# A two-layer hybrid attention trunk on one core: the second attention's low halves moved behind the matmul steps, two of its queries moved forward, and the residual's loads held back

## The chip, the core and the metric

The kernel runs on one core of a Trainium2 chip. TensorE (PE) multiplies, and its weight loads (PEld) overlap its matmuls; VectorE (DVE) and ScalarE (ACT) do the elementwise work; GpSimd (POOL) and SyncE (SP) mostly issue DMAs, and so does ACT. The metric is device time in microseconds (us). Before the change the median of three runs is 1460.07 us (1458.28 to 1465.57).

## The reference

The input is x of 512 tokens by 1024, in float32. Each of two layers computes

```
h    = rmsnorm(x) ;  proj = h @ w_in                 # queries, keys, values, gates
y_a  = forgetting_attention(q_a, k_a, v_a, f_a) @ w_o_fox        # 8 heads of 64
o_c, o_s, o_w = sparse_attention(q_b, compressed, selected, window keys and values)
y_b  = (g0 * o_c + g1 * o_s + g2 * o_w) @ w_o_nsa                # 8 heads, 2 key heads
x    = x + (sigmoid(gate_a) * y_a + sigmoid(gate_b) * y_b) @ w_out
x    = x + square(relu(rmsnorm(x) @ w_up)) @ w_down
```

and a last rmsnorm follows. Both attentions are causal. With 512 tokens the selected branch takes all eight blocks and the window covers everything, so both are plain causal attentions over different keys. Queries and the second attention's keys have a rotation of 16 of their 64 dimensions.

## The kernel before

Activations lie transposed, 128 features by 512 tokens a tile. Products in float32 are split: each operand becomes a high half (a cast) and a low half (the rest), and three matmuls give a product. A weight block of 128x1024 is fetched to `raw` (L173), cast to `wh` on ACT (L189), its low half `wl` is formed on DVE (L190), and `gemm` runs 24 matmuls of 512 columns on it (L219 to L221), six to a step; after each step the generator yields, so that other work can be put between steps. Two raw tiles and two of each half are in rotation. `order` lists all weight blocks in the order of their use. Which queue fetches them is `self.queue`: SP's, except in the second attention, where it is POOL's.

A layer goes: token projections; the first attention (`attend`), filled with the remaining projections (`fill1`: the keys and queries of the first attention, then a compression of keys and values run in turns with the rest, which ends with the selected keys `ks`, the window keys `kw`, and the first and second queries of the second attention); the second attention (`attend_pairs`); the mixing (the second output projection and the gates); the output projection, which adds x; the MLP.

The second attention is what the change touches. It has eight pairs: for each of four head pairs first the selected branch (kind 0), then the window branch (kind 1). A pair's scores (`pair_scores`) go over four row blocks, the longest first: `prepare` scales the previous block's probabilities and writes their high halves as float16 (ACT, L613); two products with the keys follow, one for each head (PE, L640), each followed by a masked maximum on DVE (L555) and an exponential on ACT (L557); `finish` forms the low halves (DVE, L618) and issues transposing DMAs on SP's queue (L623), from the half buffer `EE` to tiles `PT`. A pair later `pair_values` multiplies `PT` with the values (PE, L666 and L683). `after` adds the compressed branch and evicts (L1182 to L1191).

`attend_pairs` writes the order out by hand. Each pair has four rounds; in a round the scores advance by two yields (one block of rows), in the last two rounds the previous pair's values go out, and then `fill` advances by `rate` steps (2 in a round; 2.5 in the first pair's rounds, 3 behind the last pair). The last part of a kind 0 pair (block 0, `late`) is taken at the start of the next pair. `fill` is `fill2`: the gates' projections (a gate's product with the norm's factor on DVE, L1213, and a tanh, L1214), the first output projection, each half block of which is folded into `MA` on DVE (`ma`, L1223), and the raw projections of the third and fourth queries (`parted`). `timed` puts two more things at numbered steps: the compressed branch's probabilities (`cmp_probs`, whose last step forms `cp`, L941) and `turned(2)` and `turned(3)`, which rotate and split those two queries on DVE and ACT and copy them to `q2` by DMAs (L410).

PE's order in the stage is pinned to the order of the code. The chain of softmax, prepare and finish is tied, in code order, on DVE and on ACT. `yield_to_chain` ties each round's other DVE work (gates, `ma`, weights, `cp`) behind the last chain instruction that the round emitted before it. The rest is left to the build's scheduler.

Tiles come from pools with fixed counts: `t2` has 13 buffers (probabilities of the short rows, `PT`, `cp`, later x), `hl` one (the split keys, and the fourth row block's probabilities). The first query's copies and the selected keys' go out on SP's queue, the window keys' on POOL's. At the end of the stage the eight tiles of x are loaded on ACT's queue (L1279); nothing ties them to a place there.

## Time and profile before

| | |
|---|---|
| profiled execution | 1462.19 us; span 1460.1 us; mean granted TensorE clock 0.990 |
| busy in the span | PE 1423.4 us, DVE 1192.8 us, ACT 922.4 us, POOL 170.8 us |
| second attention, layer 0 / layer 1 | about 167 to 338 us / 889 to 1058 us |
| DVE, median of one instruction | L618 612 ns; L941 689 ns |
| transposing DMAs (L623) | 96, median issue 1278 ns |

A group line of the profile names line, engine, operation and tiles (out<-in), then how often it ran. A wait line reads: engine, what it wanted to write and its line, then who released it, with the total, the number of waits and the longest. A line of the chain gives start, duration and who was the last to hold things up; "issue" is time in which the engine waited for nothing that the profile shows. A row of the table of windows gives the stretch, its length, then busy time and instructions of PE, PEld, DVE, ACT and POOL, the granted clock, the DMA engines' share and GB/s.

### The profile page before, as it was taken

To read this page: it belongs to the slowest core of one execution; us is meant where nothing else is said; L and a number is where in the kernel's file an instruction comes from. 1 tells how busy PE (TensorE), PEld (TensorE's weight loads), DVE (VectorE), ACT (ScalarE), POOL (GpSimd) and SP (SyncE) were. 2 spreads that over 40 slices of the span, in tenths; PEclk is the share of its full clock that TensorE was granted. 3 is DMA by queue.
4 is the path that set the end of the run, shared out by engine and by line. 5 is a ranking of instruction groups with operands and counts; after the bars stand their busy time and mean duration, and the time that the engine had idled before them with its cause. 6 is when DMAs were issued, how large, how long until landed. Compare 5 with 4: busy or idle time off the path is not lost.

```text
span 1460.1 us, 23049 instructions
## 1 busy us (share of the span) xinstructions
PE 1423.4 (97%) x7948; PEld 1217.7 (83%) x7948; DVE 1192.8 (82%) x2522; ACT 922.4 (63%) x1907; POOL 170.8 (12%) x249
## 2 busy tenths in 40 slices
PE   9999999999999999999999999998899999999997
PEld 8877777777898999989888787776688989899896
DVE  6587888866889898989866878988478888989898
ACT  6375576753677575848454756767437776758485
POOL 2000101000011111111300011010000111111112
PEclk9999999999999999999999999999999999999999
DMA  7564668584558676777835646576833575766674
GB/s 254 167 158 138 152 148 157 129 158 144 154 133 197 167 180 165 193 170 202 266 134 166 180 117 167 130 159 130 167 109 114 148 182 137 197 174 176 160 213 116
DMA packets 163956, 237.67 MB, mean 163 GB/s; under 512 B 95104, under 2 KB 95488, under 8 KB 163840
## 3 DMA queue, kind: packets, MB, share of 16 engines
q1 hardware_dynamic: 137200, 162.78, 39.0%
q0 software_dynamic: 23904, 68.69, 23.2%
q10 hardware_dynamic: 2736, 4.74, 1.7%
q8 instruction: 62, 1.02, 0.3%
q14 instruction: 54, 0.44, 0.1%
HBM read 168.46 MB, written 6.29 MB: 120 GB/s over the span
## 4 chain that ended last, share of the span: by engine, by line
PE 80%; DVE 7%; DMA 5%; ACT 4%; issue 2%; SPq 0%; POOL 0%; ACTq 0%; POOLq 0%
PE ps_mm L1849 7%; PE ps_S L1849 7%; PE ps_mm L219 7%; PE ps_mm L221 7%; PE ps_mm L220 7%; PE ps_S L1722 6%; PE ps_PT L1722 6%; PE ps_mm L1722 6%; DMA PT<-EE 3%; PE ps_O L1849 3%; PE ps_PT L1849 3%; PE ps_O L1722 3%; DVE EE L618 1%; DMA q<-qs 1%; ACT EE L613 1%
## 5 line engine op out<-in xcount | busy, mean ns | idle before, releaser
L219 PE MATMUL ps_mm<-uh,wh 128*128 128x512 f32 x480 | 196.3, 409 | 16.1 <-DVE ma L1223 8.1
L221 PE MATMUL ps_mm<-uh,wl 128*128 128x512 f32 x480 | 192.1, 400 | 0.2
L220 PE MATMUL ps_mm<-ul,wh 128*128 128x512 f32 x480 | 191.2, 398 | 0.0
L189 ACT CAST wh<-raw 128x1024 fp32r<-128x1024 f32 (+2 forms) x111 | 112.4, 1013 | 116.8 <-PE ps_mm L220 41.0
L190 DVE TENSOR_TENSOR wl<-raw,wh 128x1024 fp32r<-128x1024 f32 (+2 forms) x111 | 130.4, 1176 | 38.7 <-ACT wh L189 38.3
L1831 ACT CAST sh<-raw 128x512 fp32r<-128x512 f32 x160 | 96.7, 619 | 76.2 <-DMA raw<-wt 28.0
L219 PEld LDWEIGHTS ps_mm<-uh,wh 128*128 128x128 f32 x480 | 91.8, 191 | 36.8 <-ACT wh L189 8.8
L1839 DVE TENSOR_TENSOR sl<-raw,sh 128x512 fp32r<-128x512 f32 x160 | 106.2, 684 | 18.7 <-ACT sh L1831 18.6
L221 PEld LDWEIGHTS ps_mm<-uh,wl 128*128 128x128 f32 x480 | 92.0, 192 | 21.0 <-DVE wl L190 1.6
L220 PEld LDWEIGHTS ps_mm<-ul,wh 128*128 128x128 f32 x480 | 92.4, 192 | 16.1
L1689 DVE TENSOR_TENSOR sl<-raw,sh 128x512 fp32r<-128x512 f32 x128 | 83.8, 684 | 5.2 <-ACT sh L1675 4.0
L613 ACT ACTIVATE EE<-E,rr 128x512 f16<-128x512 f32 (+3 forms) x112 | 59.3, 576 | 44.2 <-DVE rr L607 19.3
L1722 PE MATMUL ps_S<-t,sh 128*128 128x256 f32 x384 | 83.3, 283 | 1.0 <-ACT yz L1774 0.9
L1675 ACT CAST sh<-raw 128x512 fp32r<-128x512 f32 x128 | 75.2, 617 | 4.4 <-DVE sl L1839 4.4
L1675 ACT CAST sh<-sx 128x512 fp32r<-128x512 f32 x96 | 58.2, 613 | 26.6 <-DVE sx L1657 24.7
L1689 DVE TENSOR_TENSOR sl<-sx,sh 128x512 fp32r<-128x512 f32 x96 | 64.5, 684 | 12.6 <-ACT sh L1675 12.6
L557 ACT ACTIVATE E<-E,mx 128x512 f32<-128x512 f32 (+3 forms) x112 | 64.3, 575 | 15.1 <-DVE mx L555 14.7
L1722 PE MATMUL ps_S<-t,sl 128*128 128x256 f32 x256 | 72.0, 281 | 0.0
L618 DVE SCALAR_TENSOR_TENSOR EE<-E,rr,EE 128x512 f16<-128x512 f32 (+3 forms) x112 | 60.0, 575 | 11.9 <-ACT EE L613 11.6
L1696 POOL DMA_DIRECT2D raw<-raw x32 | 28.0, 874 | 342.8 <-DVE sl L1689 92.8
L219 PE MATMUL ps_mm<-oh,wh 128*128 128x512 f32 x160 | 63.6, 397 | 1.5 <-DVE gate L1213 1.2
L1825 POOL DMA_DIRECT2D raw<-wt x48 | 42.0, 879 | 195.2 <-DVE k_t L1597 87.6
(480 smaller groups left out, 4374.6 us busy)
## 6 DMA issues: line engine op xcount, KB each, us to landing
raw<-wup SPq DMA_DIRECT2D x64, 512.0 KB
raw<-wt POOLq DMA_DIRECT2D x48, 512.0 KB, 7.0
raw<-wb SPq DMA_DIRECT2D x35, 512.0 KB
raw<-wt SPq DMA_DIRECT2D x32, 512.0 KB
sx<-wt SPq DMA_DIRECT2D x64, 256.0 KB
raw<-wb POOLq DMA_DIRECT2D x29, 512.0 KB, 4.9
kd<-hl SPq DMA_DIRECT2D x40, 256.0 KB
w<-w SPq DMA_DIRECT2D x32, 256.0 KB
```

Of the source, the lines that this page charges most:

```text
L189: nc.scalar.copy(h[:, :n], raw[:, :n])
L190: nc.vector.tensor_tensor(lo[:, :n], raw[:, :n], h[:, :n].bitcast(F32), op=OP.subtract)
L219: mm(ps, h[:, c], xh, start=start and i == 0, stop=False)
L220: mm(ps, h[:, c], xl, start=False, stop=False)
L221: mm(ps, lo[:, c], xh, start=False, stop=stop and i == ks - 1)
L618: nc.vector.scalar_tensor_tensor(out[1], x, f, out[0], op0=OP.mult, op1=OP.subtract)
L1675: self.nc.scalar.copy(h, self.source(k, i))
L1689: self.nc.vector.tensor_tensor(lo, self.source(k, i), h.bitcast(F32), op=OP.subtract)
L1722: self.nc.tensor.matmul(ps, w, x, skip_group_check=True, **kw)
L1831: self.nc.scalar.copy(h, self.operand(d, i, p))
L1839: self.nc.vector.tensor_tensor(lo, self.operand(d, i, p), h.bitcast(F32), op=OP.subtract)
L1849: self.nc.tensor.matmul(ps[t][:, cols], a[:, s], m, start=new and f == 0, stop=f == 2, skip_group_check=True)
```

## The change

1. In `pair_scores` each row block yields once more ahead of `finish`. `attend_pairs` advances the scores by two as before, then the fill, and only then by one more, which runs `finish`. So the low halves and the transposes are emitted behind the round's gemm steps, and the steps' DVE work is no longer tied behind them. The same holds for the end of `late` and for the last round of a pair.
2. `fill1` takes the first query's projection ahead of `ks` and `kw`. The first pair's rows (`early`) come from `t2` rather than `hl`.
3. In `fill2` the third query's projection comes behind the first two gate blocks and their half blocks, `gated(0)`, instead of behind `gated(2)`, and `turned(2)` goes from steps 30, 32, 34 to 18, 22, 24.
4. x's loads are tied behind the last ACT instruction of `attend_pairs`. The weights' queue returns to SP's after the mixing rather than ahead of it.

```diff
--- before.py
+++ after.py
@@ -559,10 +559,13 @@
 
     def pair_rows(self, P):
 
-        X = [self.t("t2", [128, T], name="E") for _ in range(2)]
-        two = [self.t("t2", [128, T], name="E") for _ in range(2)]
-        three = self.t("hl", [128, 2, T], name="E")
-        E = [[X[e][:, :128], X[e][:, 128:384], two[e][:, :384], three[:, e]] for e in range(2)]
+        if P.get("early"):
+            three, two, X = ([self.t("t2", [128, T], name="E") for _ in range(2)] for _ in range(3))
+        else:
+            X, two = ([self.t("t2", [128, T], name="E") for _ in range(2)] for _ in range(2))
+            three = self.t("hl", [128, 2, T], name="E")
+            three = [three[:, e] for e in range(2)]
+        E = [[X[e][:, :128], X[e][:, 128:384], two[e][:, :384], three[e]] for e in range(2)]
         if P["kind"]:
             for e in range(2):
                 E[e][0] = P["first"][e]
@@ -644,6 +647,7 @@
                     self.softmax_part(mate["first"][e], ps[:, 128:256], mate["sums"][:, 4 * e:4 * e + 1])
                 if e == 0:
                     yield
+            yield
             if i < 3:
                 finish(i + 1)
             if i:
@@ -758,25 +762,26 @@
                 for g, at in plan:
                     for _ in range(at[k]):
                         next(g, None)
+                owed += rate if 0 < t < n else self.ENDS[t > 0]
+                while owed >= 1.0:
+                    owed -= 1.0
+                    next(fill, None)
                 if k == 0 and late is not None:
                     for _ in late:
                         raise AssertionError
                     late = None
+                if t < n and (k < 3 or pairs[t]["kind"] == 0):
+                    next(plan[0][0])
                 if k == 3:
                     if t < n and pairs[t]["kind"] == 0:
                         late = plan.pop(0)[0]
                     for g, _ in plan:
                         for _ in g:
                             raise AssertionError
-                owed += rate if 0 < t < n else self.ENDS[t > 0]
-                while owed >= 1.0:
-                    owed -= 1.0
-                    next(fill, None)
                 self.yield_to_chain(first)
         self.in_order(mark, (mybir.EngineType.PE,))
         for chain in self.chains:
             self.tie(chain)
-        self.queue = self.nc.sync
         run(fill)
 
     def compress(self, kc, vc, small, l):
@@ -1017,16 +1022,15 @@
             else:
                 yield flat(s), 1024
         yield from ((flat(a["wg2"][l, c]), 576) for c in self.CHUNKS[l])
-        for i in (0, 1, 2, 3, 8, 9, 4, 5, 6, 7, 10, 11, 12, 13):
+        for i in (0, 1, 2, 3, 8, 9, 4, 5, 6, 7, 12, 10, 11, 13):
             yield wb[i], 1024
         wo = [[flat(a["wo"][l, f, m]) for m in range(4)] for f in range(2)]
         for m in range(8):
             yield wb[16 + m], 1024
             if m % 2 == 1:
                 yield wo[0][m // 2], 1024
-            if m == 3:
-                yield wb[14], 1024
-                yield wb[15], 1024
+            if m in (1, 3):
+                yield wb[14 + m // 2], 1024
         yield from ((wb[24 + m], 1024) for m in range(8))
         yield from ((wo[1][m], 1024) for m in range(4))
         yield from ((flat(a["wout"][l, m]), 1024) for m in self.OUT)
@@ -1160,8 +1164,8 @@
             yield from proj(9, "vc", lambda ps: self.scaled(ps, "sx"))
             c = self.compress(st["kc"], st["vc"], small, l)
             self.kk = self.t("crs", [128, 2, 2, 2, 128], F32R, name="kk")
-            rest = chain(fox_proj(2), fox_proj(3), proj(10, "ks", lambda ps: self.k_pair(self.roped(ps), branch=0)),
-                         proj(11, "kw", lambda ps: self.k_pair(self.roped(ps), branch=1)), qproj(0), qproj(1))
+            rest = chain(fox_proj(2), fox_proj(3), qproj(0), proj(10, "ks", lambda ps: self.k_pair(self.roped(ps), branch=0)),
+                         proj(11, "kw", lambda ps: self.k_pair(self.roped(ps), branch=1)), qproj(1))
             yield from alternate(c, rest)
 
         self.pc, self.qs = {}, deque()
@@ -1196,7 +1200,7 @@
             gate = lambda br: lambda rows: gt[:, rows, br, 2 * p:2 * p + 2].rearrange("p b h -> p h b")
             b_ = dict(kind=1, ready=lambda: True, q=q, k=lambda: st["kw"][:, hk], O=O,
                       v=lambda b: VN[:, b, 2 + hk], gate=gate(2), after=after)
-            a_ = dict(kind=0, ready=lambda: ("qb", p) in st and "kw" in st, q=q, k=lambda: st["ks"][:, hk], O=O,
+            a_ = dict(kind=0, early=p == 0, ready=lambda: ("qb", p) in st and "kw" in st, q=q, k=lambda: st["ks"][:, hk], O=O,
                       v=lambda b: VN[:, b, hk], gate=gate(1), mate=b_,
                       kk=lambda: self.kk[:, :, hk].rearrange("p f b t -> p f (b t)"))
             return [a_, b_]
@@ -1224,18 +1228,16 @@
                                                op0=OP.add, op1=OP.mult)
 
         def fill2():
-            for m in (0, 2):
+            for m in (0, 2, 4, 6):
                 yield from gated(m)
-            for p in (2, 3):
-                yield from parted(p)
-            for m in (4, 6):
-                yield from gated(m)
+                if m < 4:
+                    yield from parted(2 + m // 2)
             for m in range(8):
                 yield from proj(24 + m, ("gb", m), lambda ps: gate_tanh(ps, ("oh", "ol")[m % 2]))
 
         def timed(g):
             side = {}
-            for x, at in ((self.cmp_probs(0), self.CMP[0]), (turned(2), (30, 32, 34)), (turned(3), (34, 36, 38)),
+            for x, at in ((self.cmp_probs(0), self.CMP[0]), (turned(2), (18, 22, 24)), (turned(3), (34, 36, 38)),
                           (self.cmp_probs(1), self.CMP[1])):
                 for n in at:
                     side.setdefault(n, []).append(x)
@@ -1250,6 +1252,7 @@
 
         self.attend_pairs([u for p in range(4) for u in nsa_pairs(p)], timed(fill2()), self.NSA_FILL, 6)
         yb = [st["ob", p] for p in range(4)]
+        end = self.ends()
 
 
         mixed = []
@@ -1273,10 +1276,15 @@
                 mix()
         for m in range(4):
             mix()
+        self.queue = nc.sync
         self.tail = self.ends()
         x = [self.t("t2", [128, T], name="x") for _ in range(KT)]
+        mark = len(nc.cur_bb.bb.instructions)
         for k in self.OUT:
             nc.scalar.dma_start(x[k], self.x_src[k])
+        end, self.tail = self.tail, {mybir.EngineType.Activation: end[mybir.EngineType.Activation]}
+        self.not_ahead(mark)
+        self.tail = end
         return self.mlp(l, x, mixed, self.gain[:, 16 * l + 8:16 * l + 16])
 
     OUT = (0, 4, 1, 5, 2, 6, 3, 7)
```

## The prediction

> **What bounds the kernel now.** I read the page first: the span, the busy shares and the chain of waits by engine.
>
> ```profile
> span 1460.1 us, 23049 instructions
> PE 1423.4 (97%) x7948; PEld 1217.7 (83%) x7948; DVE 1192.8 (82%) x2522; ACT 922.4 (63%) x1907; POOL 170.8 (12%) x249
> PE 80%; DVE 7%; DMA 5%; ACT 4%; issue 2%; SPq 0%; POOL 0%; ACTq 0%; POOLq 0%
> ```
>
> PE is busy 97% of the span and holds 80% of the chain, so TensorE bounds the kernel, and a change of order can only win back what PE stands idle or runs slowly. The list of PE's waits, taken for the second attention's two stages alone (160 to 345 us in layer 0, 880 to 1065 us in layer 1; columns: total us, times, longest), says how much that is. Layer 0:
>
> ```profile
> PE ps_mm L219 <- DVE ma L1223: 4.1, 2, 2.2
> PE ps_mm L219 <- ACT wh L189: 2.9, 1, 2.9
> PE ps_S L640 <- DMA q<-qs: 2.4, 1, 2.4
> PE ps_PT L640 <- DVE cp L941: 1.2, 1, 1.2
> PE ps_mm L219 <- DVE gate L1213: 0.5, 1, 0.5
> ```
>
> Layer 1:
>
> ```profile
> PE ps_mm L219 <- ACT wh L189: 5.1, 1, 5.1
> PE ps_mm L219 <- DVE ma L1223: 4.0, 2, 2.1
> PE ps_PT L640 <- DVE cp L941: 1.2, 1, 1.2
> PE ps_PT L935 <- DVE mx L555: 1.2, 1, 1.2
> PE ps_S L640 <- DMA q<-qs: 1.1, 1, 1.1
> PE ps_mm L219 <- DVE gate L1213: 0.7, 1, 0.7
> PE ps_O L666 <- DMA PT<-EE: 0.5, 1, 0.5
> ```
>
> That is 11.1 us in layer 0 and 13.8 us in layer 1, 24.9 us in all. By cause: VectorE late with an ordinary step of the round (ma 8.1, gate 1.2, cp 2.4, mx 1.2: 12.9 us), a weight not yet cast (8.0 us), the first query (3.5 us), a transpose (0.5 us).
>
> A stall also costs clock. The next rows are the table of windows, with the granted clock after POOL's column, and two lines of the chain around one stall:
>
> ```profile
> 167.30:192.40 25.10, 22.54 (x97) 18.22 (x97) 16.55 (x45) 14.32 (x36) 1.65 (x3) 0.93 0.56 136
> 192.40:208.10 15.70, 15.70 (x77) 12.40 (x76) 14.30 (x39) 11.08 (x25) 1.07 (x2) 1.00 0.58 120
> ...
> 241.70:263.60 21.90, 20.00 (x92) 15.74 (x91) 17.26 (x52) 13.96 (x38) 2.72 (x5) 0.92 0.93 174
> ...
> 280.10:300.30 20.20, 18.03 (x81) 14.16 (x80) 14.90 (x47) 14.34 (x37) 1.08 (x2) 0.92 0.71 151
> ...
> 315.40:338.00 22.60, 19.58 (x83) 14.19 (x82) 7.58 (x10) 6.75 (x11) 1.08 (x2) 0.92 0.96 209
> ```
>
> ```profile
> 990.00:1010.00 20.00, 15.96 (x66) 12.10 (x65) 16.76 (x46) 13.62 (x31) 1.61 (x3) 0.91 0.67 153
> 1050.00:1070.00 20.00, 17.52 (x69) 13.27 (x70) 9.40 (x12) 8.92 (x13) 1.07 (x2) 0.83 0.42 122
> ```
>
> ```profile
> 333.39 0.43 PE ps_mm L220
> ...
> 335.79 0.23 PE ps_mm L219
> ```
>
> Behind the last stall of layer 0 a 512-column matmul takes 0.43 us, and 2.4 us later 0.23 us again. The work lost to the low clock is at most (1 - clock) times the window: 1.8, 1.8, 1.6 and 1.8 us in layer 0, 1.8 and 3.4 us in layer 1, 12.2 us in all (an upper bound, since low clock inside a gap is free). By cause: query 1.8, ma 5.2, weight cast 5.2. So the most that this change can win is 24.9 + 12.2 = 37.1 us.
>
> The Trainium skill (TensorE: Matmul & The Clock Gate, Part 1) says that the clock halves only after an idle window of about 3.4 us. Here it fell after waits of 2.1 to 2.9 us, so the trace disagrees and I keep the rows; by the rule only the 5.1 us stall would pay its 3.4 us.
>
> **Part one, x's loads.** The list of ACT's waits in 300 to 335 us, then in 1030 to 1060 us, and two lines of the chain:
>
> ```profile
> ACT wh L189 <- DMA x<-xT: 12.6, 1, 12.6
> ```
>
> ```profile
> ACT wh L189 <- DMA x<-xs: 14.9, 1, 14.9
> ```
>
> ```profile
> 315.00 14.30 DMA PT<-EE
> ...
> 329.38 0.33 ACTq L1279
> ```
>
> The eight loads of x (256 KB each by their shape, L1279) sit in ACT's queue among the stage's last steps. One of them waits for a transpose that itself takes 14.3 us because x's 2 MB move beside it (DMA share 0.96 in the window quoted). ACT stands still 12.6 and 14.9 us, the cast of the next weight stands behind it, and PE stalls 2.9 and 5.1 us, with the clock 8.0 + 5.2 = 13.2 us. The change ties the loads behind the last ACT instruction of the stage, so nothing of the stage is queued behind them and the transposes have the DMA engines nearly alone. What is late next is the last pair's transposes themselves. The slowest one in mid-stage is this:
>
> ```profile
> 243.43 5.01 DMA PT<-EE
> 248.44 3.18 issue
> ...
> 252.46 1.41 DVE EE L618 x2
> 253.87 0.60 DVE ma L1223
> ```
>
> It was issued at 243.43, and ACT, which waited for it, could go on at 248.44 + 3.18 = 251.6: 8.2 us. The last transpose, issued about 2 us after the one of 315.00, would so land by 325.3, or by 327.2 if the deferral of part two costs 1.9 us. The products that need it come right behind the matmul of 333.39, less the stall's 4.7 us: about 329. No wait, or a short one. At the new place eight issues of 0.33 us take 2.7 us of ACT, and 2 MB move, beside the mixing:
>
> ```profile
> 340.00:360.00 20.00, 20.00 (x90) 16.57 (x89) 13.26 (x17) 6.28 (x8) 0.00 (x0) 1.00 0.28 80
> ```
>
> ACT is busy 6.28 of 20 us there and the DMA engines 0.28, and x is first used after eight half blocks of 12 matmuls and one block of 24, 120 x 0.23 = 27 us; at the 209 GB/s of the window of 315.4 us the 2 MB take 10 us. That cover is ample; without it, ACT's 2.7 us in each layer would be the price. The weights of the mixing now go out on POOL's queue rather than SP's (the queue is switched back later); POOL is idle in that window, so I cost it at nothing, up to 1 us a layer. Taken: -12.0 (bounds -8 and -13.2).
>
> **Part two, the second halves.** Today `finish` (the low halves on VectorE, then the transposes on SP's queue) is emitted ahead of the round's gemm steps, and the steps' VectorE work is tied behind it. The chain above shows the cost: ma stands behind the low halves (L618), which wait for ACT (L613), which waits for a transpose to have read its rows; and PE waits for ma's bank. Put behind the gemm steps, the low halves no longer stand ahead of ma and gate. In 192.4 to 226.4 us one of each costs (busy us, mean ns):
>
> ```profile
> L190 DVE TENSOR_TENSOR wl<-raw,wh 128x1024 fp32r<-128x1024 f32 x4 | 4.9, 1216 | 0.0
> ...
> L1223 DVE SCALAR_TENSOR_TENSOR ma<-gate,ps_mm 128x512 f32<-128x512 f32 x2 | 1.4, 685 | 0.0
> ...
> L1213 DVE TENSOR_TENSOR gate<-ps_mm,R 128x512 f32<-128x512 f32 x2 | 1.3, 652 | 0.0
> ```
>
> The bounds for all of VectorE's waits are 0 and -12.9 - 5.2 = -18.1. The waits for ma (8.1) with their clock (5.2) I take as three quarters gone, -10.0; gate and mx (2.4) as half, -1.2; cp (2.4) as staying, because its neighbourhood gets busier. The new cost: a round's low halves and transposes start later by a gate and a weight's low half, 0.65 + 1.22 = 1.9 us, and SP's queue, PE's value products and the next pair's ACT step (which overwrites the rows the transposes read) wait for them. How much room is there? For the seventh pair of layer 0:
>
> ```profile
> 293.49 5.70 SPq L623 DMA_TRANSPOSE PT<-EE  x4
> ```
>
> ```profile
> 307.92 1.47 PE L666 MATMUL ps_O<-PT,vn 128*128 128x512 f16 x6
> ```
>
> 14.4 us from first issue to use; less the 8.2 us above that leaves some 6 us. But the fourth pair of layer 1 has none: there PE already waits 0.5 us for a transpose. In layer 0 the same pair's transpose, the one of 243.43 above, is the slow one too. I charge the full 1.9 us there in each layer: +3.8 (bounds 0 and 6, with clock).
>
> **Part three, the third query sooner.** Its rotation and split are five VectorE passes over 128x512; at 0.68 us (ma's row) 3.4 us, moved from the third and fourth pair into the second. The second pair, 192.4 to 208.1, has VectorE busy 14.30 of 15.70 us, and loses about a gate and a ma (1.3 us) to the new step order, so 16.4 us of work meet 15.7 us of PE: 0.7 us over, in each layer, unless the third pair soaks it up. Its four copies leave POOL's queue sooner; nobody waits for them. Taken: +0.7 (bounds -1 and +3).
>
> **Part four, the first query.** SP's timeline and the chain before the first scores (with which the window of 167.30 us begins):
>
> ```profile
> 158.07 9.65 SPq L410 DMA_DIRECT2D q<-qs  x8
> ```
>
> ```profile
> 160.63 9.71 DMA q<-qs
> ```
>
> The first query's copy of 160.63 takes 9.71 us beside the window keys' and the second query's copies, to 170.3, and PE waits 2.4 us. Ahead of both keys, two blocks of 24 x 0.23 = 5.5 us earlier, its copies leave near 147. The selected keys move one block later and take the place that the window keys had, one block ahead of 158.07, so about 153; at the same 9.7 us they land by 163, and as PE asks at 167.3 they may even be 4 us worse than that. The pair's rows also leave the single `hl` buffer, so they needn't wait for the window keys' copies. Of 3.5 + 1.8 = 5.3 us I take -4.8 (bounds -2 and -5.3).
>
> **The sum.** -12.0 - 11.2 + 3.8 + 0.7 - 4.8 = -23.5 us. The profiled execution took 1462.2 us (span 1460.1 plus 2.1), and it lies 2.1 us above the median, 1460.1; so 1438.7 for it and 1436.6, say 1437, for the median.
>
> **Rivals.** First, waits change hands: the build may order VectorE by readiness, and a low half that is ready before a gate may stay ahead of it, so ma stays late; or ma is early and scores wait instead. Then part two gives nothing and may cost its 3.8: -12.0 - 4.8 = -16.8 to -13.0, 1443 to 1447. For it: only ma and gate are freed of the tie, nothing ties the halves behind them. Second, all goes: nothing new appears and some 35 of the 37.1 us come back, 1425. For it: transposes elsewhere have 6 us of room. Third, slower: the deferred transposes hold ACT. The next pair's first-half step (L613) waits for them, and the weight cast stands behind it in ACT's order; PE has a block of 5.5 us in hand. At 248.44 ACT waited 3.2 us already without costing PE a cast. If the halves also wait for the round's two steps (12 x 0.23 = 2.8 us) besides the 1.9, that becomes 7.9 us, 2.4 over the cover, 4 us with the clock. Parts one and four give 16.8, so it shows as slower by over 7.3 us from 6 of the 14 pair changes on; at 7 of them +28 - 16.8, 1471. Against it: no cast is late in mid-stage now. Fourth, shorter stalls leave the clock alone: then the sum loses the clock of ma (three quarters of 5.2), of the query and of layer 0's cast (1.8 each), 7.5 in all, and comes to -16.0, 1444; the 0.43 us row, behind a wait of 2.9 us, speaks against it. That is the rule of the clock gate page of the Trainium skill.
>
> **Chances.** 0.5% of 1460 is 7.3 us, about what a measurement can tell. Forecast (-17 to -30) 0.50; waits change hands 0.22; all goes 0.13; the clock left alone 0.02; a gain eaten up to within 7.3 us 0.06; slower 0.07. Of the second a tenth or two falls short of 7.3: faster 0.83, same 0.10, slower 0.07. The range runs from just past all the gain (1424) to 1454: waits that change hands (-13.0) with part one at -8 and part three at +3 would be -6.7.
>
> **What would show it.** Right: no ACT wait on x in the stage, transposes at its end back under 9 us, no query wait at the first scores, the waits for ma under 3 us, and a transpose wait of 1 to 3 us in the fourth pair. Wrong: PE's waits for casts in mid-stage, ACT's waits for transposes longer in most pairs, or a cp wait beyond 2 us. A wait of PE or VectorE on x after the stage would show part one wrong.

## The result and the profile after

The changed kernel takes 1438.53 us in the median of four runs (1438.02 to 1440.11), beside 1462.01 us (1458.28 to 1465.57) for the kernel before in the same comparison: a ratio of 0.9841, 95% interval 0.9812 to 0.9870. It is faster by 23.5 us; 1437 was forecast. The profiled execution took 1440.11 us, with a span of 1438.3 us and a mean clock of 0.994 (before: 0.990). In what follows, lines moved by three to five: L613 is now L616, L618 is L621, L623 is L626, L640 is L643, L907 is L912, L941 is L946, L1213 is L1217, L1214 is L1218 and L1223 is L1227.

The page of the changed kernel, the same three lines as were shown of the kernel before:

```profile
span 1438.3 us, 23079 instructions
PE 1413.9 (98%) x7948; PEld 1214.8 (84%) x7948; DVE 1193.8 (83%) x2522; ACT 919.8 (64%) x1907; POOL 178.2 (12%) x259
PE 88%; DVE 6%; ACT 2%; DMA 2%; issue 1%; POOL 0%; ACTq 0%; POOLq 0%
```

PE's share of the chain rose from 80 to 88%, and the share of DMAs fell from 5 to 2%. PE's waits over the whole execution (total us, times, longest):

```profile
PE ps_S L643 <- ACT sx L912: 6.8, 2, 4.2
PE ps_PT L643 <- DVE cp L946: 5.9, 2, 2.9
PE ps_mm L219 <- DVE ma L1227: 1.2, 2, 0.6
```

The waits for a cast (8.0 us), for the first query (3.5), for the gate (1.2), for mx (1.2) and for a transpose (0.5) are gone, and ma fell from 8.1 to 1.2 us. Two took their place: the wait for cp grew from 2.4 to 5.9 us, and the wait for the copy of the compressed scores to `sx` is new, 6.8 us. In the two stages the waits went from 24.9 to 13.9 us.

The record of the clock has TensorE at full speed or at half, and at half for 3.41 us at a time or for two or three times that. In the two stages there are seven such half-speed stretches before (counting a double one as two) and four after. At 1.7 us lost in each that is up to 5.1 us. With the 11.0 us of waits it makes 16.1 of the 21.8 us between the two spans; the other 5.7 us stand in neither list.

The end of the stage, by ACT's waits in 280 to 330 us (layer 0):

```profile
ACT wh L189 <- PE ps_mm L220: 10.4, 4, 5.3
```

and in 1000 to 1045 us (layer 1):

```profile
ACT wh L189 <- PE ps_mm L220: 11.1, 4, 5.3
```

No wait on x is left. The casts now wait for PE to be done with the buffer, so ACT is ahead of PE. From issue to the last completion, the stage's last transpose took 5.00 us in layer 0 and 6.11 us in layer 1, worked out from the records of the semaphores; before, the last two of each layer took 14.3 to 16.5 us.

The first query, by SP's timeline in 136 to 172 us:

```profile
145.05 2.40 SPq L410 DMA_DIRECT2D q<-qs  x4
...
162.60 4.80 SPq L410 DMA_DIRECT2D q<-qs  x4
```

The first query's four copies leave at 145.05, about where the prediction put them (147), and only the second query's four leave late (162.60).

The new wait for cp, by the chain of waits of the changed kernel in 198 to 214 us:

```profile
199.15 0.60 DVE tmp L354
...
200.35 0.60 DVE tmp L355
...
206.33 0.68 DVE cp L946
...
207.74 1.13 DVE wl L190
...
208.90 0.70 DVE cp L946
...
209.74 0.98 PE ps_PT L643 x2
```

The passes of `turned(2)` (L354, L355) now lie among those of the compressed branch. cp's first subtraction comes at 206.33 and its second, behind a gate and a weight, at 208.90; only then has the bank been read, and PE, which had nothing else in its order, goes on at 209.74 after 2.93 us.

The new wait for `sx`, by the chain in 240 to 262 us:

```profile
241.39 7.15 DMA PT<-EE
...
249.32 0.70 ACT EE L616
...
251.22 0.48 ACT sx L912
...
251.74 0.80 PE ps_S L643 x2
...
255.98 0.43 PE ps_mm L219
```

A transpose holds the step that will overwrite its rows (L616). The copy out of the compressed scores' bank stands behind that step on ACT, and PE needs that bank for its next scores. PE then runs at half pace for some 5 us. ACT's timeline shows that the order of the two differs, and the length of the hold, 6.52 us and 3.27 (start, duration, in brackets the idle time ahead). Changed kernel:

```profile
248.69 1.33 ACT L616 ACTIVATE EE<-E,rr 128x512 f16<-128x512 f32 x2 [6.52 <-DMA PT<-EE]
...
251.13 0.56 ACT L912 COPY sx<-ps_S 128x512 f32<-128x512 f32 x1
```

Kernel before, where the copy is done before ACT waits:

```profile
247.87 0.57 ACT L907 COPY sx<-ps_S 128x512 f32<-128x512 f32 x1
251.71 1.33 ACT L613 ACTIVATE EE<-E,rr 128x512 f16<-128x512 f32 x2 [3.27 <-issue]
```

### The profile page after: what moved, and what is told of

It reads as the page before. It is cut to its first block, busy times and chain, and to the rows that moved or that the text cites. A ratio compares the mean times of both kernels' runs of the same rounds, so it can differ in the third digit from the quotient of the medians.

```text
span 1438.3 us, 23079 instructions
## 1 busy us (share of the span) xinstructions
PE 1413.9 (98%) x7948; PEld 1214.8 (84%) x7948; DVE 1193.8 (83%) x2522; ACT 919.8 (64%) x1907; POOL 178.2 (12%) x259
## 4 chain that ended last, share of the span: by engine, by line
PE 88%; DVE 6%; ACT 2%; DMA 2%; issue 1%; POOL 0%; ACTq 0%; POOLq 0%
PE ps_mm L219 9%; PE ps_mm L221 9%; PE ps_mm L220 9%; PE ps_mm L1857 8%; PE ps_S L1857 7%; PE ps_S L1730 6%; PE ps_PT L1730 6%; PE ps_mm L1730 5%; PE ps_O L1857 3%; PE ps_PT L1857 3%; PE ps_O L1730 3%; PE ps_O L670 2%; PE ps_O L497 1%; PE ps_PT L476 1%; PE ps_S L643 1%
## 5 line engine op out<-in xcount | busy, mean ns | idle before, releaser
L219 PE MATMUL ps_mm<-uh,wh 128*128 128x512 f32 x480 | 193.4, 403 | 1.2 <-DVE ma L1227 1.2
L221 PE MATMUL ps_mm<-uh,wl 128*128 128x512 f32 x480 | 188.8, 393 | 0.0
L190 DVE TENSOR_TENSOR wl<-raw,wh 128x1024 fp32r<-128x1024 f32 (+2 forms) x111 | 130.4, 1175 | 17.3 <-ACT wh L189 17.1
L220 PEld LDWEIGHTS ps_mm<-ul,wh 128*128 128x128 f32 x480 | 90.7, 189 | 15.7
L616 ACT ACTIVATE EE<-E,rr 128x512 f16<-128x512 f32 (+3 forms) x112 | 59.3, 576 | 50.5 <-issue 18.5
L621 DVE SCALAR_TENSOR_TENSOR EE<-E,rr,EE 128x512 f16<-128x512 f32 (+3 forms) x112 | 60.6, 575 | 12.7 <-ACT EE L616 12.6
L1730 PEld LDWEIGHTS ps_S<-t,sh 128*128 128x128 f32 x384 | 63.5, 189 | 1.3 <-ACT yz L1782 1.3
```

The source lines that it names most:

```text
L190: nc.vector.tensor_tensor(lo[:, :n], raw[:, :n], h[:, :n].bitcast(F32), op=OP.subtract)
L219: mm(ps, h[:, c], xh, start=start and i == 0, stop=False)
L220: mm(ps, h[:, c], xl, start=False, stop=False)
L221: mm(ps, lo[:, c], xh, start=False, stop=stop and i == ks - 1)
L1730: self.nc.tensor.matmul(ps, w, x, skip_group_check=True, **kw)
```

## The experiments

The theory going in was the prediction's sum, with x's loads, the second halves and the first query as gains and the third query as nearly free. The first four kernels make one part of the change each, in the kernel before; their kernel before had a median of 1462.1 us. Times are medians of four to twelve runs, and a gain in us is (1 - ratio) x 1462. The diffs are cut to the lines that matter; the notes behind # and the dots are this text's.

**x's loads alone.** The kernel before, with:

```diff
-        self.queue = self.nc.sync        # at the end of attend_pairs
+        end = self.ends()                # behind attend_pairs
+        self.queue = nc.sync             # behind the mixing
         for k in self.OUT:
             nc.scalar.dma_start(x[k], self.x_src[k])
+        end, self.tail = self.tail, {mybir.EngineType.Activation: end[mybir.EngineType.Activation]}
+        self.not_ahead(mark)
+        self.tail = end
```

> Only x's loads are held back behind the stage's last ScalarE instruction (and the weights' queue is switched back later); all else as before. My theory, parts that add up: both late casts (8.0 us) and their clock (5.2 us) go, 12 to 13 us faster, ratio near 0.9915. Rival, the last pair's transposes are the real end of the stage: PE then waits for them instead of for the cast, and less than 5 us is won. In the trace: no wait of a cast on x in either layer by my theory, and a wait of PE on PT of 2 us or more behind each stage by the rival.

Measured: 1444.84 us, ratio 0.9883 (0.9854 to 0.9911), 17.1 us faster. PE's waits:

```profile
PE ps_mm L219 <- DVE ma L1222: 8.1, 4, 2.1
PE ps_S L640 <- DMA q<-qs: 3.4, 2, 2.2
```

The gain is above the 12 to 13 us expected. The waits for a cast are gone; of the others only the one for mx (1.2 us) went too (cp stays at 2.4 us). The cause given for the stall at the end of the stage is shown: one edit that touches only x's loads and the weights' queue removes it. Which of these two does it, no run parts; that ACT stood waiting for x speaks for the loads.

**The second halves alone.** The kernel before, with:

```diff
+            yield
             if i < 3:
                 finish(i + 1)
...
+                # the round's fill steps first, then:
+                if t < n and (k < 3 or pairs[t]["kind"] == 0):
+                    next(plan[0][0])
```

> Only the low halves and transposes are put behind the round's gemm steps. My theory: the waits for ma, gate and mx shrink by some 11 us with their clock and the later transposes cost up to 4 us, so 7 to 11 us faster, ratio 0.9925 to 0.995. Rival, waits change hands: the later transposes hold ScalarE and through it PE, and the gain is below 3 us (ratio above 0.998). In the trace: ma below 3 us by both; a ScalarE wait on PT of over 4 us in the fifth pair, with a PE wait behind it, by the rival.

Measured: 1448.86 us, ratio 0.9909 (0.9877 to 0.9940), 13.3 us faster. PE's waits:

```profile
PE ps_O L667 <- DMA PT<-EE: 9.1, 3, 7.4
PE ps_PT L938 <- DVE mx L555: 3.1, 2, 1.7
```

The gain is above the 7 to 11 us expected. The waits for ma and for the gate are gone altogether, and the one for mx grew from 1.2 to 3.1 us. At the end of layer 1 x's loads now hold a transpose for 17.56 us, and PE waits for the transpose itself:

```profile
1023.03 17.56 DMA PT<-EE
```

In layer 0 the stall at the end (2.9 us) is gone although nothing was done about it; in layer 1 it grew from 5.1 to 7.4 us. Where x's loads fall among the last transposes depends on a shift of a few us, for better and for worse.

**The first query alone.** The kernel before, with:

```diff
-        for i in (0, 1, 2, 3, 8, 9, 4, 5, 6, 7, 10, 11, 12, 13):
+        for i in (0, 1, 2, 3, 8, 9, 4, 5, 6, 7, 12, 10, 11, 13):
-            rest = chain(fox_proj(2), fox_proj(3), proj(10, ...), proj(11, ...), qproj(0), qproj(1))
+            rest = chain(fox_proj(2), fox_proj(3), qproj(0), proj(10, ...), proj(11, ...), qproj(1))
+        if P.get("early"):               # the first pair's rows from t2, not hl
```

> Only the first query's projection goes ahead of the keys' and the first pair's rows leave the shared buffer. My theory: 3.5 us of waits and 1.8 us of clock go, 4 to 5 us faster, ratio near 0.9967. Rival, the keys' copies become the late ones: below 1.5 us, with PE or VectorE waiting on kd at the first scores.

Measured: 1452.73 us, ratio 0.9932 (0.9909 to 0.9955), 9.9 us faster. PE's waits:

```profile
PE ps_mm L219 <- DVE ma L1226: 8.1, 4, 2.2
PE ps_O L669 <- DMA PT<-EE: 6.5, 3, 3.6
```

The wait for the query (3.5 us) is gone. The stall at the end changed hands and size again: at most 6.5 us for transposes where 8.0 us for casts stood; the wait for the gate grew from 1.2 to 3.3 us. In all the waits are only 2.8 us shorter, and there are two half-speed stretches fewer, up to 3.4 us. One of these belongs to the query; the other stood behind a wait for ma, which is as long as before (2.17 and 2.13 us). So what lies above the 5.3 us that the query could give is in part chance, and in part not in these lists; no run parts it.

**The third query alone.** The kernel before, with:

```diff
-            for m in (0, 2):
-                yield from gated(m)
-            for p in (2, 3):
-                yield from parted(p)
-            for m in (4, 6):
+            for m in (0, 2, 4, 6):
                 yield from gated(m)
+                if m < 4:
+                    yield from parted(2 + m // 2)
-            (turned(2), (30, 32, 34))
+            (turned(2), (18, 22, 24))
```

> Only the third query's projection and its rotation go earlier. My theory from the record: about nothing, 0.7 us slower. After the changed kernel's profile I add a second one: VectorE is full in the second and third pair, so the wait for cp grows from 1.2 to about 3 us in each layer, and this part alone is 2 to 5 us slower, unless it also cuts the wait for ma in the fifth pair (1.9 us a layer), when it comes out even.

Measured: 1467.13 us, ratio 1.0031 (1.0012 to 1.0049), slower by 4.5 us. PE's waits:

```profile
PE ps_PT L640 <- DVE cp L941: 7.1, 2, 3.5
PE ps_mm L219 <- ACT wh L189: 5.6, 1, 5.6
PE ps_S L640 <- ACT sx L907: 4.4, 2, 2.5
```

Both new waits of the changed kernel, for cp and for `sx`, are here, without the second halves: they belong to this part. The second of the two theories, written after the changed kernel's profile, held. ma has halved by itself (4.3 us), and at the stage's end the cast wait of layer 0 grew from 2.9 to 5.6 us, while in layer 1 2.4 us for a transpose stand in its place. In all the waits grew by 3.0 us, and there are ten half-speed stretches instead of seven.

The next three were run together on another chip (kernel before: 1462.68 us).

**The change without the third query.** The changed kernel, with the diff above taken back.

> The changed kernel with the third query back at its old place (projection behind the second group of gates, rotation at steps 30, 32, 34). My theory after the four parts alone: the third part is a loss, since with it the wait for cp is 2.9 us a layer instead of 1.2 and ScalarE's copy sx stands behind a held-up step (4.2 and 2.6 us). Without it 8 to 14 us faster than the changed kernel: 1425 to 1431 us, no wait for sx, cp below 1.3 us a wait. Rival, the third part belongs to the second: with the halves late and the query's copies back beside the fourth pair's transposes, PE waits for PT or sx there anyway, and the time is that of the changed kernel, 1436 to 1442.

Measured: 1429.26 us, ratio 0.9792 (0.9760 to 0.9823), against 0.9841 (0.9812 to 0.9870) for the whole change: without this part it is faster by 0.0049 x 1462 = 7.2 us, though the two intervals touch. PE's waits:

```profile
PE ps_PT L940 <- DVE mx L555: 3.0, 2, 1.5
PE ps_O L670 <- DMA PT<-EE: 2.1, 2, 1.1
PE ps_PT L643 <- DVE cp L946: 1.8, 2, 0.9
```

The wait for `sx` is gone, and cp is down from 5.9 to 1.8 us. The wait for mx is back, at 3.0 us. No wait is longer than 1.5 us, neither stage has a half-speed stretch, and the mean clock is 0.998, where the change has 0.994. A transpose wait of 1.0 and 1.1 us, one in each layer (before: 0.5 us in layer 1), is the small cost of the deferral that the prediction had charged.

**The change without the second halves.** The changed kernel, with `finish` ahead of the fill again, in `attend_pairs` too.

```diff
-            yield
             if i < 3:
                 finish(i + 1)
```

> The changed kernel with the low halves back ahead of the gemm steps. My theory: the waits for ma and gate come back (about 4 us a layer with the clock, less what the third part already takes in the fifth pair), 8 to 12 us slower than the changed kernel, 1446 to 1450 us. Rival, the gain of the halves is already in the other parts: within 3 us of the changed kernel.

Measured: 1449.59 us, ratio 0.9920 (0.9896 to 0.9944): within the change this part is worth 0.0079 x 1462 = 11.5 us. cp is at 7.0, `sx` at 4.8, ma at 4.3 and the gate at 2.7 us. The new waits stand without the second halves, too.

**The compressed branch's steps moved, in both groups.** The changed kernel, with:

```diff
-    CMP = (14, 17, 19, 20, 21, 25), (43, 45, 47, 48, 49, 53)
+    CMP = (8, 11, 13, 14, 15, 17), (45, 47, 49, 50, 51, 55)
```

> The changed kernel with the compressed branch's steps moved: the first group from (14, 17, 19, 20, 21, 25) to (8, 11, 13, 14, 15, 17), out of the second pair into the first, the second group two steps later, (45, 47, 49, 50, 51, 55), so that sx is not emitted in the round in which ScalarE is held. My theory: the cp wait (5.9 us in both layers) came from VectorE being full in the second pair and goes; the sx wait (6.8 us) was one of place and goes; with the clock 14 to 18 us faster than the changed kernel, 1421 to 1425 us. Rivals: VectorE is full in the first pair as well and the wait turns up there (cp or mx, 2 us or more); or the hold on ScalarE shows up at the next cast instead of sx, with a PE wait on wh of 2 us or more in the fifth pair.

Measured: 1438.69 us, ratio 0.9845 (0.9815 to 0.9876), as the change itself. cp fell to 2.0 us and `sx` went, but others came:

```profile
PE ps_O L670 <- DMA PT<-EE: 7.6, 6, 2.5
PE ps_S L908 <- DVE mx L555: 2.8, 1, 2.8
```

The theory that these two waits would simply go if their steps stood six steps earlier and two later fell; the rival, that the wait turns up elsewhere, held. That the branch's VectorE work now meets other pairs' low halves, whose transposes then come late, is likely, but it was not tried by itself.

The next four ran together (kernel before: 1460.14 us).

**The change once more**, unchanged, as the measure for these.

> The changed kernel itself once more, beside the three others on one chip. Theory and rival alike: 1436 to 1442 us.

Measured: 1434.25 us, ratio 0.9822 (0.9805 to 0.9839), 1.8 us below the expected range. cp is at 5.8 us; the wait for `sx` came in one layer only (3.2 us). So this wait is not the same in each execution. Against this run the kernel without the third query is ahead by 0.0030 x 1462 = 4.4 us only, which the intervals alone don't tell from nothing; the two waits, and the clock behind them, speak for a cost.

**The second group's first step three earlier.** The changed kernel, with:

```diff
-    CMP = (14, 17, 19, 20, 21, 25), (43, 45, 47, 48, 49, 53)
+    CMP = (14, 17, 19, 20, 21, 25), (40, 45, 47, 48, 49, 53)
```

> The changed kernel with only the first step of the second compressed group (the matmuls into the S bank and ScalarE's copy sx) moved from step 43 to step 40, into the round before. Theory: the wait of 4.2 and 2.6 us for sx is one of place, because the copy stands in ScalarE's order behind a step that waits for the fourth pair's transposes; the copy goes ahead of it, the wait and its clock go, 8 to 10 us faster than the changed kernel, 1428 to 1431 us, while the cp waits (2.9 each) stay. Rival: the hold on ScalarE by the transposes is the cause, whatever stands behind it; PE then waits for wh, ma or a softmax in the fifth pair instead, and the time is within 3 us of the changed kernel.

Measured: 1430.56 us, ratio 0.9794 (0.9779 to 0.9809), 3.7 us less than the change beside it, where 8 to 10 were expected; that run had only one of the two waits for `sx`, and the two intervals touch. ACT's timeline:

```profile
239.44 0.56 ACT L912 COPY sx<-ps_S 128x512 f32<-128x512 f32 x1
...
245.86 1.34 ACT L616 ACTIVATE EE<-E,rr 128x512 f16<-128x512 f32 x2 [1.86 <-DVE mx L555]
```

The copy stands ahead of the held step again and the wait for it is gone, while cp stays at 5.8 us. But more than the place changed: the step itself now waits 1.86 us, for a maximum, and not 6.52 us for a transpose. In the unchanged order PE's wait goes with the length of this hold: 4.20 us for 6.52, 3.20 for 5.53 and 2.59 for 4.79. In layer 1 of the change once more the copy stands behind the step, too, the hold is short, and PE doesn't wait for the copy:

```profile
957.24 1.34 ACT L616 ACTIVATE EE<-E,rr 128x512 f16<-128x512 f32 x2 [2.41 <-DVE ma L1227]
```

So the wait for `sx` takes both, the place behind the step and a long hold. That an earlier copy removes it is shown; which of the two it removes it by is not.

**The change without x's part.** The changed kernel, with the first experiment's lines taken back.

> The changed kernel with x's loads free again and the weights' queue switched back as before. If the parts simply add up: 17 us slower than the changed kernel (what the part won alone), 1455. My theory after the halves alone and the query alone: with the halves late or the first pair's rows in other buffers the loads happen to hold ScalarE behind a cast instead of ahead of it, and PE waits for the last transposes, so the part is worth only about half here: 6 to 11 us slower, 1445 to 1449 us.

Measured: 1450.84 us, ratio 0.9932 (0.9909 to 0.9955), 16.6 us more than the change beside it. PE waits 14.1 us for transposes in the two layers, and ACT, in 300 to 335 us:

```profile
ACT wh L189 <- DMA x<-xT: 10.9, 1, 10.9
```

The stall that this part removes is larger beside the deferred transposes (14.1 us) than it was in the kernel before (8.0 us), in one profile, that of the longest of the six runs. My theory at that point, that half of its value had already come with the other parts, fell; plain addition, 17 us, was right for this part.

**The change without the third query, two steps moved.** The kernel without the third query, with:

```diff
-    CMP = (14, 17, 19, 20, 21, 25), (43, 45, 47, 48, 49, 53)
+    CMP = (14, 17, 19, 20, 21, 23), (43, 45, 47, 48, 49, 55)
```

> The changed kernel without the third query's part, and the last step of each compressed group moved into a fourth round of a window pair, where no scores use the PT banks (step 25 to 23, step 53 to 55). Theory: there the waits for cp (0.9 each) and mx (1.5 each) are waits for a PT bank, and go: 4 to 6 us faster than the kernel without the third part, 1423 to 1426 us. Rival: VectorE is full in those pairs and another of its steps becomes late: within 2 us of that kernel, 1427 to 1431 us.

Measured: 1430.63 us, ratio 0.9799 (0.9781 to 0.9816), no different from 0.9792 (0.9760 to 0.9823): the rival held. The waits for cp and mx that were aimed at went, but others came at the second group (an exponential 2.7 us, cp 2.5, a transpose 2.2). This edit gives nothing on that kernel.

**The whole change with one step of each group moved.** From these, the changed kernel, third query and all, with:

```diff
-    CMP = (14, 17, 19, 20, 21, 25), (43, 45, 47, 48, 49, 53)
+    CMP = (14, 17, 19, 20, 21, 23), (40, 45, 47, 48, 49, 53)
```

> The changed kernel, third part kept, with two steps of the compressed branch moved: sx from step 43 to 40 as before, and the step that forms cp from 25 to 23, into the fourth round of the second pair, where no scores use the PT banks. Theory: the cp wait (2.9 us a layer, with the clock some 3.5) is one of place too: PE asks for the bank two rounds later and finds it free; 5 to 7 us faster than with sx alone, 1423 to 1426 us, the fastest of all. Rival: VectorE is full in the second pair and is late with cp wherever it stands; then the same wait stays, or turns up at another bank, and the time is 1429 to 1432 us.

Measured: 1427.36 us (1426.83 to 1428.02), against a kernel before of 1460.41, ratio 0.9778 (0.9752 to 0.9804). It lies between the expectation and the rival, and it is the lowest time of the study; its interval overlaps those of the kernel without the third query and of the one with only `sx` moved. Against the latter it gains 2.3 us by the ratios, where 5 to 7 were expected. PE's waits:

```profile
PE ps_PT L643 <- DVE cp L946: 2.5, 2, 1.3
PE ps_PT L940 <- DVE sx L935: 1.8, 2, 0.9
```

What else is left is 0.8 us for a step of `prepare` and 0.6 us for transposes, 5.7 us in all; without the third query it was 6.9. The third query's passes are all still in the second pair. So its cost in the change is no plain surplus of VectorE work; it came with where the compressed branch's steps stand beside it. (What these two moves give without the third query was not tried.) PE's timeline shows how cp's wait shrank. Changed kernel:

```profile
203.12 0.60 PE L940 MATMUL ps_PT<-ct,sx 128*128 128x128 f32 x4
...
209.74 0.98 PE L643 MATMUL ps_PT<-kd,q 128*128 128x384 f32 x2 [2.93 <-DVE cp L946]
```

This kernel:

```profile
200.89 0.63 PE L940 MATMUL ps_PT<-ct,sx 128*128 128x128 f32 x4 [0.89 <-DVE sx L935]
...
209.55 0.59 PE L643 MATMUL ps_PT<-kd,q 128*128 128x384 f32 x2 [1.29 <-DVE cp L946]
```

VectorE is done with cp at nearly the same time, 209.60 and 209.40, so it is late wherever the step stands, as the rival had it. PE asks for the bank at 208.26 instead of 206.81. This execution runs 0.40 us later from the values before on (198.96 and 198.56), and PE has already stood 0.89 us for `sx`, ahead of the transposes into the bank (L940), which now come before the scores of the round. So one wait of 2.93 us became two, 0.89 and 1.29 us, and neither stage has a half-speed stretch. The theory that PE finds the bank free fell. Against the kernel with only `sx` moved, the waits of the two stages are 1.3 us shorter in all, and two half-speed stretches, up to 3.4 us, are gone: most of what this edit gives is clock.

## Why the prediction was right, and where its steps were not

The total, 1438.7 for the profiled execution and 1437 for the median, met 1440.1 and 1438.5. It did so through errors that cancel, so that it came this close is luck; that it is faster, and by what in the main, is not.

**Part one, x's loads: -12.0.** The mechanism is shown in both directions. The size was probably too small: alone the part gave 17.1 us, with an interval of 13.0 to 21.3, which just reaches the bound of 13.2, and within the change 16.1 by the ratios. Within the change, the step that failed is the one that took the stall from the trace of before: there it had grown from 8.0 to 14.1 us. The deferral of part two, which the prediction itself adds to the last transpose's time, is the likely reason, but it was not tried by itself. Alone, the profile has 9.4 us of waits and three half-speed stretches less, 14.5 us together; the rest is in no list. The eight loads at the new place cost PE nothing that its list of waits shows.

**Part two, -11.2 and +3.8.** Three quarters of the ma waits were taken as gone; alone the part removed all 8.1 us of them, and the gate's. mx was taken as half gone, and with this part alone it grew, from 1.2 to 3.1 us. The charge of 3.8 us for transposes in the fourth pair is what failed: in the changed kernel PE does not wait for a transpose at all, and in the kernel without the third query 2.1 us are left of it, for both layers. Net -7.4 was forecast, -11.5 us measured within the change.

**Part three, +0.7.** This is the term that was most wrong. It cost 4.5 us alone (interval 1.8 to 7.2) and 4.4 to 7.2 us within the change, above its bound of +3 each time, though no interval shuts that out. The step set 16.4 us of VectorE work against 15.7 us of PE, a surplus in bulk. What decided was not the bulk but the order. cp's subtractions, for which PE holds a bank, were queued behind the new passes, and the build put another order on ACT, in which the copy to `sx` stands behind a step held by a transpose. The forecast let cp stay at 2.4 us "because its neighbourhood gets busier"; the same words gave the reason for it to grow. The prediction's own sign for being wrong, a cp wait beyond 2 us, came true at 2.9. With two steps moved the kernel with the query's passes is as fast as the one without them, as the last run shows.

**Part four, -4.8.** The wait of 3.5 us is gone in every kernel that has the edit, and the copies left near the time worked out. Alone it measured 9.9 us, with part of that from the stage's end. Taken from the whole, 23.2 - 16.1 - 11.5 + 7.2 (all by ratios) leaves 2.8 us for it; with the 4.4 us of the repeated measurement for the third query nothing is left. No run took it out of the change, so its share stays open between nothing and about 5 us.

**The rivals.** The first, that waits change hands, came in part: 6.8 us for `sx` and 3.5 us more for cp stand where ma and the cast had been, but by part three and not, as it had it, because low halves stay ahead of the gate. The third, deferred transposes that hold ACT, was seen at work in its mechanism: ACT stood 6.52 us for one. It hit the copy to `sx` in place of the cast, at one place in a layer and not at six of 14, so its price was 3 to 7 us in waits and not 28. It was also not the deferral that did it, since the wait stands at 4.8 us without the second halves. "All goes", 1425 us, is nearly what the last run reached, 1427.36, with the compressed branch's steps set to fit.

**The parts do not add.** Alone they gave -17.1, -13.3, -9.9 and +4.5, -35.8 together, where the change gave -23.2 by the same measure. x's part is worth about the same in both (17.1 and 16.1). So the surplus lies among the other three: -18.7 as a sum, -9.9 in the change without x's part. What the profiles show of it is the stall at the stage's end. It stands at 8.0 us before, at 7.4 with the halves alone, at most 6.5 with the first query and 8.0 with the third, but at 14.1 us with the three together. Why it grows, and whether that is all of the surplus, stays open.

**The clock.** The changed kernel's windows in layer 0:

```profile
200.00:210.00 10.00, 7.07 (x34) 5.68 (x33) 9.27 (x23) 6.28 (x13) 2.66 (x5) 0.96 0.92 196
210.00:226.00 16.00, 16.00 (x74) 12.79 (x74) 12.60 (x40) 12.83 (x34) 0.55 (x1) 0.92 0.68 150
240.00:262.00 22.00, 17.80 (x78) 13.60 (x78) 13.57 (x40) 11.11 (x31) 1.12 (x2) 0.84 0.73 132
```

Clock still costs up to 0.4 + 1.3 + 3.5 = 5.2 us there; in layer 1 one stretch is left, up to 1.7 us, behind a wait of 2.59 us for `sx`. The fourth rival, that shorter stalls leave the clock alone, is contradicted in layer 0: behind the 2.93 us of waiting up to 209.74 the clock is 0.92 over the next 16 us. By the rule of the Trainium skill (TensorE: Matmul & The Clock Gate, Part 1) it should take an idle window of about 3.4 us; the trace does not agree. Nor do waits have to reach the 2.1 us that the prediction names as the shortest: in the kernel before, the one of 1.90 us lowered the clock as well (the last section has the row).

## What to carry to other kernels

When an edit moves work into a stretch that is nearly full, don't weigh busy time against length alone: go through what stands in order on each engine there, and ask which bank or buffer the bound engine wants next and what now stands ahead of its release. A stall that comes from transfers meeting by chance moves with any shift of a few us, so measure an edit against a kernel without that stall before its gain is believed. Where an edit loses although its work is small, move the neighbouring steps by two or three places before giving it up; here a shift of six places only moved the waits elsewhere. A long wait cut into short ones, as 2.93 us into 0.89 and 1.29 here, can save more by the clock than by the waiting.

## What was not expected of the hardware

The same wait had two outcomes for the clock. In layer 1 of the changed kernel PE waited for cp for 2.93 us as in layer 0, and the clock stayed full. The records of the clock tell why. In one trace the half-speed stretches begin whole multiples of 3.413 us apart (in the changed kernel at 209.19, 250.15 and 963.54 us, 12 and 209 such steps). So the traces can be cut into windows of that step, and what counts is how long PE stands idle in one of them. In layer 0 one window has 2.38 us of the wait, and the next one is at half speed; in layer 1 the wait falls on two windows, 1.78 and 1.15 us:

```profile
205.78:209.19 3.41, 1.03 (x5) 0.59 (x4) 3.32 (x6) 2.67 (x6) 0.00 (x0) 1.00 1.16 228
209.19:212.60 3.41, 2.86 (x7) 2.46 (x8) 3.15 (x10) 2.46 (x6) 0.57 (x1) 0.50 0.65 168
...
919.17:922.58 3.41, 1.63 (x8) 1.11 (x6) 3.35 (x7) 2.73 (x6) 0.00 (x0) 1.00 1.12 181
922.58:926.00 3.42, 2.27 (x11) 1.97 (x12) 3.29 (x10) 1.22 (x2) 0.57 (x1) 1.00 1.01 209
```

Shorter waits part in the same way. One of 1.94 us in the kernel with the third query alone is cut into 0.66 and 1.28 us by the windows, and the clock stays full (1.00 over the window from 255.20 and the next). One of 1.90 us in the kernel before lies in one window:

```profile
252.53:255.95 3.42, 1.52 (x7) 1.19 (x7) 3.09 (x10) 3.42 (x8) 0.00 (x0) 1.00 0.56 156
255.95:259.36 3.41, 3.41 (x12) 2.73 (x10) 3.41 (x6) 1.23 (x5) 0.00 (x0) 0.50 0.41 78
```

Over the fourteen traces of this study (the first 6 and the last 9 us of each left out), every window at full speed with 2.02 us or more of idle PE was followed by a half-speed one, and none with 1.78 us or less. Of the seven between 1.80 and 1.93 us, five were. So no wait of up to 1.8 us cost clock by itself, one of 2 to 3 us did or did not by where it fell, and 0.89 and 1.29 us in place of 2.93 were safe. Why the bound lies there, no run shows.

A transpose from SBUF to SBUF depends on what moves beside it. From issue to landing (from the records of the semaphores) the last four of each stage took 2.4 to 6.1 us in the changed kernel, and the very last one 15.3 to 18.4 us in the kernel before and in the change without x's part, where x's 2 MB move among them.
